# Sums of half activations in a hybrid attention block: joined parts, and parts that follow one and two pieces later

## The chip, the cores and the metric

The kernel runs on one core of a Trainium2 chip. The metric is the device time of one execution in microseconds (us). Five engines work side by side, each through its own queue in order: TensorE (PE, matmuls; its weight loads are PEld), VectorE (DVE), ScalarE (ACT), GpSimd (POOL) and SyncE (SP). SP issues the loads of weights, POOL most other transfers. Line numbers such as L147 are those of the kernel before.

## The reference

One layer of a decoder block on 512 positions of width 2048, all in float32. Cut to what matters:

```
h    = rms_norm(x, norm_g)
proj = h @ w_in                       # q, kv, gate logits, z_a, uv, z_b, merge logits
o_a  = nsa_attention(q, kv, gates) * silu(z_a)
u, v = split(gelu(uv))
o_b  = u * (tril(w_s) @ layer_norm(v) + b_s) * silu(z_b)
g_a, g_b = split(sigmoid(merge_logits))
merged = g_a * (o_a @ w_up_a) + g_b * (o_b @ w_up_b)
x    = x + merged @ w_out
x    = x + sigmoid(x @ w_ple_gate) * (p @ w_ple)
out  = rms_norm(x, final_g)
```

## The kernel before

**Two parts per number.** TensorE multiplies float32 operands rounded to fp32r. To keep the accuracy, each operand is split into a high part (the rounded value, a cast by ScalarE, `high`, L141) and a low part (what is left, a subtraction by VectorE, `low`, L147), and each product is three matmuls: high x high, high x low, low x high.

**Two kinds of jobs.** A plain job (kinds "N" and "T") multiplies the activations with a block of weights in pieces, one piece for each 128 rows of weights (in u and wo). A job of kind "S" multiplies two column blocks of 512 at once with seven products of halves instead of eight. These need sums and differences of halves: of the weights (VectorE, L240, in the stream) and of the activations. With first and second half of the 2048 channels (k1, k2) and of each 512 positions' tile (lo_t, hi_t, 256 wide), the activation sums are s1 = (k1, hi_t) + (k2, hi_t), s2 = s1 - (k1, lo_t), s3 = (k1, lo_t) - (k1, hi_t), and s4 = (k2, lo_t) - s2. s1 lies as product "5" in `ob_h`, s2 as "6" in `ob_l`, s4 as "3" in two tiles `s40` and `s41`; s3 is staged in a tile `stage`, stored to DRAM (`s3_dram`) and loaded later over the (hi_t) halves of the activations.

**The stream.** `gemm` (L288) is a generator that emits the matmuls of all jobs in order: pl, kc, vc, k, vs, vw, q and za, then u0, u1 (plain), vn, zb, m0 to m3, ua (S), ub, wo0, wo1 (plain), wo2 (S), pg (plain). At the head of each piece it calls `flush()`, which runs what was put on the list `deferred`, then `split_to`, which emits the high parts of the weights up to three pieces ahead and the low parts two pieces ahead, and then `pop()`, which takes items from the queue `background`: `state["pops"]` items per piece, on average. What runs during `flush` and is put on `deferred` again comes at the next piece's head. `fill(n)` advances the stream by n quarter pieces, `finish(name)` to the end of a job, with a flush.

**The work around the change.** The sums are background items, first while u0 and u1 run (on h), and again while wo0 and wo1 run (on merged). `sum_chunk(c)` (L1201) makes s1, s2 and s3 of two of the eight channel tiles, c from 0 to 3, in seven items; `s4_chunk(c)` (L1246) s4 in three. All read high and low parts of the activations as separate operands. In the first use the items of `sum_chunk` alternate with those of `oa_chunk` (L1172), which makes the sums for the job ua from the attention's output and stores them to `oa_dram` through a ring of three tiles (tag "hs"). Parts are made inside the item that makes the sum: `split`, or `high` and then `low` in the next item. Rings of tiles in the pool `quad`: "s1" (two tiles, the sums), "ls" (three: `oas`, `stage`, and the low parts of S jobs), "hs" (three: `oa`, and the high parts of S jobs).

Rates: two items per piece in u (L1269), 1.5 for the s4 items behind them (L1302), 1.75 in wo (L1472). Between the first items the masked spatial weights are made: `wn` is loaded, turned by TensorE (L1282), masked (L1283) and stored (L1286), and `bn` is turned (L1288).

In wo0's end VectorE adds the result to x (L675); TensorE turns the sums (L1490) for the job pg.

Of the kernel before, what the change touches and what calls it, by code (L numbers as in the profile page):

```python
# [4 lines left out]

# [1 line left out]

# [6 lines left out]
F32 = mybir.dt.float32  # L14
F32R = mybir.dt.float32r
# [48 lines left out]
def kernel(ctx: ExitStack, tc: tile.TileContext, x, p, norm_g, w_in,  # L64
# [54 lines left out]
    def act_h(k, sl=slice(None)):  # L119
        return act_part("h", k, sl)  # L120
# [1051 lines left out]
    def oa_chunk(c):  # L1172

        f1, f2 = o32[:, c], o32[:, c + 4]
        lo_t, hi_t = slice(0, 256), slice(256, 512)
        w = {}

        def put(src, i, n):
            o = quad["pool"].tile([P, 2, S], F32R, tag="hs", name="oa", bufs=3)[:, :, :256 * n]
            split(o[:, 0], o[:, 1], src, 0.5)  # L1180
            for j in range(n):
                nc.gpsimd.dma_start(oa_dram[:, i + j, :, c], o[:, :, 256 * j:256 * j + 256])
# [18 lines left out]
    def sum_chunk(c):  # L1201

        lo_t, hi_t = slice(0, 256), slice(256, 512)
        k1, k2 = slice(2 * c, 2 * c + 2), slice(2 * c + 8, 2 * c + 10)
        h11, l11, h21, l21 = (a(k1, t) for t in (lo_t, hi_t) for a in (act_h, act_l))
        h12, l12, h22, l22 = (a(k2, t) for t in (lo_t, hi_t) for a in (act_h, act_l))
        w = {}

        def op(a, b, f):
            nc.vector.tensor_tensor(out=w["t"], in0=a.bitcast(F32) if a is not None else w["t"],  # L1210
                                    in1=b.bitcast(F32) if b is not None else w["t"], op=f)

        def first():
            w["t"] = quad["pool"].tile([P, 2, 256], F32, tag="s1", name="sum", bufs=2)
            op(h21, h22, ALU.add)
            op(None, l21, ALU.add)

        def s1():
            op(None, l22, ALU.add)
            split(sum_part("5", k1, lo_t), sum_part("5", k1, hi_t), w["t"])  # L1220

        def s2():
            op(None, h11, ALU.subtract)
            op(None, l11, ALU.subtract)
            high(sum_part("6", k1, lo_t), w["t"])

        def s2_low():
            low(sum_part("6", k1, lo_t), sum_part("6", k1, hi_t), w["t"])

        def s3():  # L1230
            w["t"] = quad["pool"].tile([P, 2, 256], F32, tag="s1", name="sum", bufs=2)
            op(h11, h21, ALU.subtract)
            op(None, l11, ALU.add)

        def s3_high():
            op(None, l21, ALU.subtract)
            w["o"] = quad["pool"].tile([P, 2, S], F32R, tag="ls", name="stage", bufs=3)
            high(w["o"][:, :, lo_t], w["t"])

        def s3_low():  # L1240
            low(w["o"][:, :, lo_t], w["o"][:, :, hi_t], w["t"])
            for i, t in enumerate((lo_t, hi_t)):
                nc.gpsimd.dma_start(s3_dram[:, i, k1], w["o"][:, :, t])
        return [first, s1, s2, s2_low, s3, s3_high, s3_low]

    def s4_chunk(c):  # L1246
        k1, k2 = slice(2 * c, 2 * c + 2), slice(2 * c + 8, 2 * c + 10)
        lo_t, hi_t = slice(0, 256), slice(256, 512)
        w = {}

        def first():
            t = w["t"] = quad["pool"].tile([P, 2, 256], F32, tag="s1", name="sum", bufs=2)
            h12, l12, h, l = (a.bitcast(F32) for a in (act_h(k2, lo_t), act_l(k2, lo_t),
                                                       sum_part("6", k1, lo_t), sum_part("6", k1, hi_t)))
            nc.vector.tensor_tensor(out=t, in0=h12, in1=h, op=ALU.subtract)
            nc.vector.tensor_tensor(out=t, in0=t, in1=l, op=ALU.subtract)
            w["l"] = l12
# [12 lines left out]
    wn, ws = (quad["pool"].tile([P, 8, P], F32, tag="ls", name=n, bufs=3) for n in ("wn", "ws"))  # L1270
    tri = mix["pool"].tile([P, P], F32, tag="v", name="tri", bufs=2)
    bn = mix["pool"].tile([8, P], F32, tag="v", name="bn", bufs=2)
    nc.sync.dma_start(wn, sgu_w.rearrange("g t s -> t g s"))
    nc.sync.dma_start(bn, sgu_b)
    nc.gpsimd.memset(tri, 1.0)
    nc.gpsimd.affine_select(out=tri, in_=tri, pattern=[[1, P]], compare_op=ALU.is_ge, fill=0.0,
                            base=0, channel_multiplier=-1)
    fill(16)
    for hf in range(2):
        b = bank("s", "ps_w")  # L1280
        for j in range(4):
            nc.tensor.transpose(b[:, j * P:j * P + P], wn[:, 4 * hf + j], ident)  # L1282
        nc.vector.tensor_tensor(out=ws[:, 4 * hf:4 * hf + 4], in0=b.rearrange("p (g t) -> p g t", g=4),  # L1283
                                in1=tri.unsqueeze(1).to_broadcast([P, 4, P]), op=ALU.mult)
        fill(4)
    nc.gpsimd.dma_start(ws_dram, ws)  # L1286
    b = bank("s", "ps_b")
    nc.tensor.transpose(b[:, :8], bn, ident[:8, :8])  # L1288
    nc.vector.tensor_copy(sgu_bt, b[:, :8])
# [292 lines left out]
```

## Time and profile before

| what | us |
|---|---|
| median of 3 runs (1576.57 to 1576.93) | 1576.73 |
| the profiled execution's own time | 1576.64 |
| its span, first to last instruction | 1574.9 |
| TensorE busy | 1559.2 |
| VectorE busy | 1108.6 |
| ScalarE busy | 743.7 |
| GpSimd busy | 230.7 |

The page gives for each engine its busy time, then the chain of work that ended last, followed back from the end. Other views: busy time by stage (a window in us from the span's start, its length, and for each engine busy time and count of instructions, then the granted TensorE clock, the share of time that the DMA engines were busy, and GB/s); waits (who waited for whom: total us, times, longest); timelines (start, us, engine, line, operation, output<-input, count, and in brackets the idle time before it and what ended it); groups of instructions by line (count, busy us, mean ns, idle time before); and transfers (count, KB each, median us from issue to landing). u0 and u1 run from 490.7 to 579.4 us of the span, vn to 656.5, zb to 732.7; wo0 and wo1 from 1217.3 to 1309.8, then wo2.

### The profile page before, as it was taken

What the parts mean: (1) busy time and instruction counts of PE and PEld (TensorE: products, weight loads), DVE (VectorE), ACT (ScalarE), POOL (GpSimd) and SP (SyncE); (2) the same over time, 40 slices, a digit from 0 to 9 for tenths busy, and PEclk for the clock granted to TensorE, in tenths of its full rate; (3) what the DMA queues carried; (4) which work ended last, traced back from release to release, by engine and by line L of the source; (5) the groups of instructions that cost most, each with busy time, mean ns of one, the idle gap of its engine ahead of it and who ended that gap; (6) DMA issues with size and microseconds to landing.
All of it is one profiled execution on the core that took longest, in us unless ns stands there. A gap on an engine that the chain in (4) does not pass through costs nothing.

```text
span 1574.9 us, 20483 instructions
## 1 busy us (share of the span) xinstructions
PE 1559.2 (99%) x7534; PEld 1304.6 (83%) x7534; DVE 1108.6 (70%) x1795; ACT 743.7 (47%) x1307; POOL 230.7 (15%) x344
## 2 busy tenths in 40 slices
PE   9999999999999999999999999999999999999997
PEld 7889988888888888888888888888888878888886
DVE  6543358889887787878887777777576687843336
ACT  7433346666664445445544444454322334433334
POOL 1200000101112420001121212110032111011111
PEclk9999999999999999999999999999999999999999
DMA  9422431112114992526473737674733476573443
GB/s 326 120 80 84 113 81 43 53 41 54 46 50 124 264 315 87 200 64 230 142 254 120 253 103 267 241 269 155 291 112 94 133 249 205 171 283 99 156 147 134
DMA packets 152916, 246.16 MB, mean 156 GB/s; under 512 B 8280, under 2 KB 78576, under 8 KB 150384
## 3 DMA queue, kind: packets, MB, share of 16 engines
q1 hardware_dynamic: 114768, 150.00, 30.6%
q0 software_dynamic: 37904, 94.49, 17.7%
q8 instruction: 59, 0.97, 0.2%
q14 instruction: 41, 0.34, 0.1%
q10 hardware_dynamic: 144, 0.36, 0.1%
HBM read 197.11 MB, written 47.71 MB: 155 GB/s over the span
## 4 chain that ended last, share of the span: by engine, by line
PE 90%; DVE 6%; ACT 2%; DMA 1%; issue 1%; SPq 0%; DVEq 0%; POOL 0%; ACTq 0%; POOLq 0%
PE ps_m L311 6%; PE ps_m L312 6%; PE ps_m L313 6%; PE ps_pg L351 3%; PE ps_pg L349 3%; PE ps_pg L350 3%; PE ps_za L337 2%; PE ps_za L339 2%; PE ps_t L1019 2%; PE ps_za L338 2%; PE ps_ub L351 2%; PE ps_ub L350 2%; PE ps_ub L349 2%; PE ps_wo L313 2%; PE ps_ua L313 2%; PE ps_zb L313 2%
## 5 line engine op out<-in xcount | busy, mean ns | idle before, releaser
L147 DVE TENSOR_TENSOR lo<-raw,hi 128x512 fp32r<-128x512 f32 (+1 forms) x280 | 195.1, 702 | 174.4 <-PE ps_pg L350 81.7
L141 ACT CAST hi<-raw 128x512 fp32r<-128x512 f32 (+1 forms) x280 | 168.7, 610 | 251.9 <-PE ps_pg L351 95.9
L147 DVE TENSOR_TENSOR ls<-b,hs 128x1024 fp32r<-128x1024 f32 x160 | 195.9, 1224 | 105.8 <-ACT hs L141 105.0
L141 ACT CAST hs<-b 128x1024 fp32r<-128x1024 f32 x160 | 168.0, 1053 | 191.1 <-PE ps_m L313 88.3
L141 ACT CAST hs<-raw 128x1024 fp32r<-128x1024 f32 x64 | 67.5, 1054 | 82.7 <-PE ps_m L313 35.2
L311 PE MATMUL ps_m<-hs,act_h 128*128 128x512 f32 x256 | 100.5, 393 | 0.0
L312 PE MATMUL ps_m<-ls,act_h 128*128 128x512 f32 x256 | 99.7, 389 | 0.0
L313 PE MATMUL ps_m<-hs,act_l 128*128 128x512 f32 x256 | 99.6, 389 | 0.0
L147 DVE TENSOR_TENSOR ls<-raw,hs 128x1024 fp32r<-128x1024 f32 x64 | 78.3, 1223 | 14.6 <-ACT hs L141 14.5
L141 ACT CAST pth<-ps_t 128x512 fp32r<-128x512 f32 (+1 forms) x88 | 48.0, 546 | 65.5 <-PE ps_t L1019 65.2
L240 DVE TENSOR_TENSOR b<-b,b 128x1024 f32<-128x1024 f32 x64 | 78.0, 1219 | 0.0
L240 DVE TENSOR_TENSOR b<-raw,b 128x1024 f32<-128x1024 f32 x64 | 78.0, 1218 | 0.0
L980 ACT ACTIVATE prob<-prob,st 128x512 f32<-128x512 f32 (+3 forms) x128 | 70.7, 556 | 4.0 <-DVE st L971 3.8
L147 DVE TENSOR_TENSOR ptl<-ps_t,pth 128x512 fp32r<-128x512 f32 (+1 forms) x88 | 56.3, 639 | 21.1 <-ACT pth L141 20.3
L971 DVE CUSTOM_DVE_ANT_0 prob<-ps_s,b 128x512 f32<-128x512 f32 (+3 forms) x128 | 56.3, 486 | 10.0 <-PE ps_s L968 9.8
L313 PEld LDWEIGHTS ps_m<-hs,act_l 128*128 128x128 f32 x256 | 48.1, 188 | 10.1
L311 PEld LDWEIGHTS ps_m<-hs,act_h 128*128 128x128 f32 x256 | 48.1, 188 | 9.8
L312 PEld LDWEIGHTS ps_m<-ls,act_h 128*128 128x128 f32 x256 | 48.1, 188 | 9.7
L337 PE MATMUL ps_za<-act_h,hi 128*128 128x512 f32 x128 | 55.8, 436 | 0.0
L337 PE MATMUL ps_q<-act_h,hi 128*128 128x512 f32 x128 | 53.6, 419 | 0.0
L1019 PEld LDWEIGHTS ps_t<-ident,prob 128*128 128x128 f32 x320 | 39.7, 140 | 13.9 <-DVE ptl L147 2.8
L350 PE MATMUL ps_wo<-lo,act_h 128*128 128x512 f32 x128 | 49.9, 390 | 1.2 <-DVE lo L147 1.2
(511 smaller groups left out, 4361.9 us busy)
## 6 DMA issues: line engine op xcount, KB each, us to landing
raw<-in_w_in_dram SPq DMA_DIRECT2D x116, 512.0 KB, 3.7
b<-in_w_in_dram SPq DMA_DIRECT2D x48, 512.0 KB, 5.6
raw<-in_w_ple_gate_dram SPq DMA_DIRECT2D x32, 512.0 KB, 3.6
raw<-in_w_out_dram SPq DMA_DIRECT2D x24, 512.0 KB, 3.8
raw<-in_w_up_b_dram SPq DMA_DIRECT2D x16, 512.0 KB, 3.7
oa_d<-oa POOLq DMA_DIRECT2D x28, 256.0 KB, 3.6
gate<-keep POOLq DMA_DIRECT2D x24, 256.0 KB, 3.8
xt<-in_x_dram SPq DMA_DIRECT2D x4, 1024.0 KB, 10.1
```

The source lines that it names most:

```text
L141: nc.scalar.copy(hi, src)
L147: nc.vector.tensor_tensor(out=lo, in0=src, in1=hi.bitcast(F32), op=ALU.subtract)
L240: nc.vector.tensor_tensor(out=b[o], in0=b[x], in1=b[y], op=ALU.subtract)
L311: nc.tensor.matmul(o, ah, hi[:, i], start=st, stop=False, skip_group_check=go)
L312: nc.tensor.matmul(o, ah, lo[:, i], start=False, stop=False, skip_group_check=go)
L313: nc.tensor.matmul(o, al, hi[:, i], start=False, stop=sp, skip_group_check=go)
L337: nc.tensor.matmul(ps, hi[:, j], ah, start=st, stop=False)
L349: nc.tensor.matmul(o, ah[:, sl], hi[:, j], start=st, stop=False)
L350: nc.tensor.matmul(o, ah[:, sl], lo[:, j], start=False, stop=False)
L351: nc.tensor.matmul(o, al[:, sl], hi[:, j], start=False, stop=sp)
L980: nc.scalar.activation(sl, sl, AF.Exp, bias=st[:, 0, j, hh:hh + 1], scale=-1.0, accum_out=st[:, 1, j, hh:hh + 1])
L1019: nc.tensor.transpose(b[:, (2 * e + hh) * P:(2 * e + hh + 1) * P], pts[hh][:, c:c + P], ident)
```

## The change

Sums are made from joined parts: `whole` first adds high and low parts of the k1 halves into one tile of tag "ls", and s1, s2 and s3 start from there. In wo a chunk has four items, the last of which makes s4 from s2's sum while it is still whole; in u `sum_chunk` has three items and `s4_chunk` two. The parts of a sum are made by `parts_later`: the high part at the head of the next piece, the low part (and the store of `stage`) at the head of the one after. In `oa_chunk` the high part is made in the item, the low part and the store at the next head. The queue in u is two `oa` items and one sum item in turn, 1.6 a piece, then 1.2 for the s4 items; in wo it is 0.7. Four flushes follow the last item in u. `wn` and `ws` are each two tiles of half the size in the rings of the pool `mix`, stored in two halves, and `bn` lies in a tile of the ring "s1" and is turned before `wn`.

```diff
@@ oa_chunk
         def put(src, i, n):
             o = quad["pool"].tile([P, 2, S], F32R, tag="hs", name="oa", bufs=3)[:, :, :256 * n]
-            split(o[:, 0], o[:, 1], src, 0.5)
-            for j in range(n):
-                nc.gpsimd.dma_start(oa_dram[:, i + j, :, c], o[:, :, 256 * j:256 * j + 256])
+            split(o[:, 0], o[:, 1], src, 0.5, later=True)
+
+            def store():
+                for j in range(n):
+                    nc.gpsimd.dma_start(oa_dram[:, i + j, :, c], o[:, :, 256 * j:256 * j + 256])
+            deferred.append(store)
@@ new helpers
+    def parts_later(hi, lo, src, then=None):
+
+        def second():
+            low(hi, lo, src)
+            if then:
+                then()
+
+        def first():
+            high(hi, src)
+            deferred.append(second)
+        deferred.append(first)
+
+    def new_sum():
+        return quad["pool"].tile([P, 2, 256], F32, tag="s1", name="sum", bufs=2)
@@ sum_chunk
-        return [first, s1, s2, s2_low, s3, s3_high, s3_low]
+        def whole():
+            t = w["t"] = quad["pool"].tile([P, 4, 256], F32, tag="ls", name="whole", bufs=3)
+            add(t[:, 0:2], act_h(k1, hi_t), act_l(k1, hi_t))
+            add(t[:, 2:4], act_h(k1, lo_t), act_l(k1, lo_t))
+
+        def s1():
+            o = w["1"] = new_sum()
+            add(o, w["t"][:, 0:2], act_h(k2, hi_t))
+            add(o, o, act_l(k2, hi_t))
+            parts_later(sum_part("5", k1, lo_t), sum_part("5", k1, hi_t), o, lambda: w.update(ready=True))
+
+        def s23():
+            o, t = new_sum(), w["t"]
+            w["2"] = o
+            sub(o, w["1"], t[:, 2:4])
+            sub(t[:, 2:4], t[:, 2:4], t[:, 0:2])
+            parts_later(sum_part("6", k1, lo_t), sum_part("6", k1, hi_t), o)
+            st = quad["pool"].tile([P, 2, S], F32R, tag="ls", name="stage", bufs=3)
+
+            def store():
+                for i, t in enumerate((lo_t, hi_t)):
+                    nc.gpsimd.dma_start(s3_dram[:, i, k1], st[:, :, t])
+            parts_later(st[:, :, lo_t], st[:, :, hi_t], t[:, 2:4], store)
+
+        def s4():
+            assert w["ready"]
+            o = w["1"]
+            sub(o, act_h(k2, lo_t), w["2"])
+            add(o, o, act_l(k2, lo_t))
+            parts_later(sum_part("3", k1, lo_t), sum_part("3", k1, hi_t), o)
+        return [whole, s1, s23] + fourth * [s4]
@@ s4_chunk
         def second():
-            nc.vector.tensor_tensor(out=w["t"], in0=w["t"], in1=w["l"], op=ALU.add)
-            high(sum_part("3", k1, lo_t), w["t"])
-
-        def third():
-            low(sum_part("3", k1, lo_t), sum_part("3", k1, hi_t), w["t"])
-        return [first, second, third]
-
-    for pair in zip_longest(*([f for c in range(4) for f in g(c)] for g in (oa_chunk, sum_chunk))):
-        background.extend(f for f in pair if f)
-    state["pops"] = 2
+            o = w["o"]
+            add(o, o, act_l(k2, lo_t))
+            parts_later(sum_part("3", k1, lo_t), sum_part("3", k1, hi_t), o)
+        return [first, second]
+
+    oa_items = [f for c in range(4) for f in oa_chunk(c)]
+    sum_items = [f for c in range(4) for f in sum_chunk(c, False)]
+    for i in range(12):
+        background.extend(oa_items[2 * i:2 * i + 2] + sum_items[i:i + 1])
+    state["pops"] = 1.6
@@ behind it
+    for hf in range(2):
+        nc.sync.dma_start(wn[hf], sgu_w[4 * hf:4 * hf + 4].rearrange("g t s -> t g s"))
     nc.sync.dma_start(bn, sgu_b)
...
     fill(16)
+    b = bank("s", "ps_b")
+    nc.tensor.transpose(b[:, :8], bn, ident[:8, :8])
+    nc.vector.tensor_copy(sgu_bt, b[:, :8])
+    fill(4)
...
     while background:
         fill(1)
+    for _ in range(4):
+        flush()
...
-    state["pops"] = 1.5
+    state["pops"] = 1.2
...
-    for f in (sum_chunk, s4_chunk):
-        for c in range(4):
-            background.extend(f(c))
-    state["pops"] = 1.75
+    for c in range(4):
+        background.extend(sum_chunk(c))
+    state["pops"] = 0.7
```

More of the change, by code (lines that the diff above doesn't have):

```diff
@@ L1204, in sum_chunk @@
+    def new_sum():
+        return quad["pool"].tile([P, 2, 256], F32, tag="s1", name="sum", bufs=2)
+    def sum_chunk(c, fourth=True):
         k1, k2 = slice(2 * c, 2 * c + 2), slice(2 * c + 8, 2 * c + 10)
-        h11, l11, h21, l21 = (a(k1, t) for t in (lo_t, hi_t) for a in (act_h, act_l))
-        h12, l12, h22, l22 = (a(k2, t) for t in (lo_t, hi_t) for a in (act_h, act_l))
         w = {}
-        def op(a, b, f):
-            nc.vector.tensor_tensor(out=w["t"], in0=a.bitcast(F32) if a is not None else w["t"],
-                                    in1=b.bitcast(F32) if b is not None else w["t"], op=f)
@@ L1213, in first @@
[L1213 to L1216, printed above, removed]
-        def s1():
[L1219 to L1243, printed above, removed]
@@ L1271 @@
[L1271 to L1273 removed]
+            o = w["o"] = new_sum()
+            sub(o, act_h(k2, lo_t), sum_part("6", k1, lo_t))
+            sub(o, o, sum_part("6", k1, hi_t))
+        def second():
+            o = w["o"]
+            add(o, o, act_l(k2, lo_t))
+            parts_later(sum_part("3", k1, lo_t), sum_part("3", k1, hi_t), o)
@@ new lines, in s4_chunk @@
+        return [first, second]
[4 more added lines that the diff above has]
+    state["pops"] = 1.6
+    wn, ws = ([mix["pool"].tile([P, 4, P], F32, tag=tags[i], name=n, bufs=2 if tags == "vv" else 1) for i in range(2)]
+              for n, tags in (("wn", "vv"), ("ws", ("g0", "g1"))))
+    tri = mix["pool"].tile([P, P], F32, tag="w", name="tri")
```

27 lines of the change are left out of this document (10 added, 17 removed).

## The prediction

> **What bounds the kernel now.** I read the page first, then busy time by stage, the waits of TensorE, and the timelines around those waits. The page:
>
> ```profile
> span 1574.9 us, 20483 instructions
> ...
> PE 90%; DVE 6%; ACT 2%; DMA 1%; issue 1%; SPq 0%; DVEq 0%; POOL 0%; ACTq 0%; POOLq 0%
> ```
>
> TensorE sets the end, and the order of its instructions stays (three small groups of transposes excepted). So the change can only win what TensorE now loses in the stages where the sums are made: u0 and u1, with their tail in vn (first use), and wo0 and wo1 (second use). The table of stages (window, its length, then each engine's busy time):
>
> ```profile
> 490.70:579.40 88.70, 88.70 (x395) 73.10 (x394) 73.14 (x124) 38.38 (x67) 30.95 (x45) 1.00 0.94 273
> 579.40:656.50 77.10, 76.48 (x337) 62.99 (x336) 61.60 (x61) 38.04 (x45) 7.40 (x12) 1.00 0.51 157
> 656.50:732.70 76.20, 76.20 (x338) 63.08 (x337) 60.09 (x58) 37.00 (x43) 4.32 (x8) 1.00 0.43 139
> 1217.30:1309.80 92.50, 91.21 (x418) 75.34 (x418) 72.45 (x110) 33.21 (x56) 15.87 (x19) 1.00 0.66 213
> ```
>
> u has no idle time at all. vn (77.10) is 0.9 longer than zb (76.20), which has the same matmuls. wo has 1.3 idle. The waits of TensorE in 480 to 735 us and in 1200 to 1400 us are these two:
>
> ```profile
> PE ps_vn L312 <- DVE ls L147: 0.6, 1, 0.6
> ...
> PE ps_wo L350 <- DVE lo L147: 1.2, 1, 1.2
> ```
>
> A busy matmul is 0.39 but the next starts 0.23 later, so the price of a stall is its step from start to start less 0.23. TensorE's timeline at the three places where it loses time:
>
> ```profile
> 590.28 0.39 PE L311 MATMUL ps_vn<-hs,act_h 128*128 128x512 f32 x1
> 591.30 0.50 PE L312 MATMUL ps_vn<-ls,act_h 128*128 128x512 f32 x1 [0.62 <-DVE ls L147]
> 591.64 0.40 PE L313 MATMUL ps_vn<-hs,act_l 128*128 128x512 f32 x1
> ...
> 1266.74 1.33 PE L1490 MATMUL ps_x<-ident,x 128*128 128x128 f32 x8
> ...
> 1273.37 1.03 PE L1490 MATMUL ps_x<-ident,x 128*128 128x128 f32 x8
> ...
> 1281.06 0.39 PE L349 MATMUL ps_wo<-hi,act_h 128*128 128x512 f32 x1
> 1282.65 0.50 PE L350 MATMUL ps_wo<-lo,act_h 128*128 128x512 f32 x1 [1.21 <-DVE lo L147]
> 1282.98 0.39 PE L351 MATMUL ps_wo<-hi,act_l 128*128 128x512 f32 x1
> ```
>
> vn: 1.02 - 0.23 = 0.79, and 0.34 - 0.23 = 0.11 in the step after it: 0.90. The first transposes of x take 1.33 where the next eight take 1.03: 0.30. wo1: 1.59 - 0.23 = 1.36, and 0.33 - 0.23 = 0.10: 1.46. Together 2.66 us. That is all there is to win.
>
> Who is late at these places? VectorE, behind the sums (L1210, L1255 to L1264), and it is late because it waits inside them: each sum's high part is cast by ScalarE at once, and the low part, next in VectorE's queue, waits for that. VectorE, then ScalarE:
>
> ```profile
> 588.28 0.69 DVE L147 TENSOR_TENSOR s<-sum,s 128x512 fp32r<-128x512 f32 x1 [0.69 <-ACT s L141]
> 588.89 1.22 DVE L240 TENSOR_TENSOR b<-b,b 128x1024 f32<-128x1024 f32 x1
> 590.02 2.50 DVE L147 TENSOR_TENSOR ls<-b,hs 128x1024 fp32r<-128x1024 f32 x2
> ...
> 1278.84 0.69 DVE L1210 TENSOR_TENSOR sum<-sum,act_l 128x512 f32<-128x512 f32 x1
> 1280.71 1.29 DVE L147 TENSOR_TENSOR x2t<-ps_x,x2t 128x512 fp32r<-128x512 f32 x2 [1.17 <-ACT x2t L141]
> 1281.91 0.68 DVE L147 TENSOR_TENSOR lo<-raw,hi 128x512 fp32r<-128x512 f32 x1
> ...
> 1279.57 0.62 ACT L141 CAST ob_l<-sum 128x512 fp32r<-128x512 f32 x1 [2.21 <-DVE sum L1210]
> 1280.09 1.07 ACT L141 CAST x2t<-ps_x 128x512 fp32r<-128x512 f32 x2
> ```
>
> At 1279.57 ScalarE has idled 2.21 for a sum; the two x2t casts stand behind it, VectorE waits 1.17 for those, and `lo`, which TensorE needs at 1281.3, starts at 1281.91. At 588.28 the low part of `s` comes after 0.69 of waiting, then L240 and two `ls`, the second of which TensorE needs at 590.5.
>
> **The change part by part.** First, the instructions. A chunk had 11 VectorE sums (8 in `sum_chunk`, 3 in `s4_chunk`). In wo it now has 8 (two each in `whole`, `s1`, `s23`, `s4`); in u it has 9, since `s4_chunk` keeps its 3. With four chunks: 8 fewer in u, 12 fewer in wo. The price of one, and of the low and high parts, whose number stays:
>
> ```profile
> L1210 DVE TENSOR_TENSOR sum<-sum,act_l 128x512 f32<-128x512 f32 x20 | 13.8, 690 | 0.4
> L147 DVE TENSOR_TENSOR lo<-raw,hi 128x512 fp32r<-128x512 f32 x31 | 21.2, 685 | 0.0
> L141 ACT CAST hi<-raw 128x512 fp32r<-128x512 f32 x29 | 17.5, 618 | 8.2 <-PE ps_u L351 5.5 <-issue 1.6 <-ACT hi L141 1.0
> ```
>
> 8 x 0.69 = 5.5 us of VectorE in u, 12 x 0.69 = 8.3 in wo.
>
> Second, the waits. `parts_later` puts the cast at the head of the next piece of the stream and the low part at the head of the one after. VectorE's waits for parts, first from u and vn, then from wo (where `ob_h` has the same row):
>
> ```profile
> DVE ob_h L147 <- ACT ob_h L141: 2.8, 4, 0.7
> DVE s L147 <- ACT s L141: 2.8, 4, 0.7
> DVE stage L147 <- ACT stage L141: 0.7, 1, 0.7
> ...
> DVE stage L147 <- ACT stage L141: 2.8, 4, 0.7
> DVE s L147 <- ACT s L141: 1.4, 2, 0.7
> ```
>
> 6.3 us in u, 7.0 in wo. The length of a piece, from u's matmuls (128 of this line, four to a piece):
>
> ```profile
> L349 PE MATMUL ps_u<-hi,act_h x128: 389/389/504, 491.0 to 578.7; 128*128 128x512 f32 x128
> ```
>
> 87.7 / 127 x 4 = 2.76 us, against a cast of 0.62: the part is there long before VectorE asks. The casts no longer wait on ScalarE either, because the sum was issued a piece earlier. One exception: after the last item of u four flushes follow each other at once, so up to three parts still wait, 0.7 each; `lo` is two pieces (5.5) ahead of TensorE, which hides it.
>
> So VectorE gets back 11.8 us in u and 15.3 in wo, in stages where it was busy 73.1 of 88.7 and 72.5 of 92.5 beside its waits. In wo1 the `lo` that came 0.6 late and held TensorE for 1.36 comes several us earlier: I take the whole 1.46. The adds of x (L675) no longer stand in a queue that runs late, so the transposes find them done: 0.30. In vn the tail goes: the items at 1.6 a piece are done after 36 / 1.6 = 22.5 pieces (before: 52 / 2 = 26), and the eight s4 items at 1.2 take 6.7 more, 29.2 of the 32 pieces of u0 and u1 (before: 26 + 8 = 34, two of them in vn). What is late next there is VectorE's own `ls` work, 3 x 1.22 = 3.7 us in each two pieces of 5.5, which keeps up in zb without a stall: 0.90. Sum: -2.66.
>
> Third, what is moved. On POOL's queue the stores of `oa` and `stage` come one and two pieces later, and the ws store is two of half the size; on SP's queue wn is two loads, ahead of weights that wait for a buffer anyway. The prices of the stores, from the page, from the burst of weights at 564 us, and from a quiet stretch at 1286 us; then the weights of wo2's burst, and one issue of two stores:
>
> ```profile
> oa_d<-oa POOLq DMA_DIRECT2D x28, 256.0 KB, 3.6
> ...
> s_d<-stage POOLq DMA_DIRECT2D x2, 256.0 KB, 7.4
> ...
> s_d<-stage POOLq DMA_DIRECT2D x2, 256.0 KB, 3.1
> ...
> b<-in_w_out_dram SPq DMA_DIRECT2D x8, 512.0 KB, 11.8
> ...
> 505.21 1.43 POOL L1182 DMA_DIRECT2D oa_d<-oa  x2 [5.52 <-DVE oa L149]
> ```
>
> Where the change adds a wait: an `oa` tile (tag hs, three of them) is held a piece longer, 2.76 until its low part, 0.7 for that, 1.4 to issue, and the landing: h = 4.9 + landing. The next high part of `oa` waits on ScalarE for such a tile, with the casts of the weights queued behind it, and TensorE waits for those. Sixteen tiles go through three places in 16 / 3 x h; the items give them 22.5 x 2.76 = 62.1 us, and `lo` is 5.5 ahead, so TensorE pays when 5.33 h is over 67.6, at a mean landing of 7.8. At 3.6, 5.33 h is 45.3: cost nothing, with 22 us of cover. At 11.8 for every store it is 89.0: cost 21.4. I take the 3.6, which is the median of these very stores in u, and keep the other end for a rival.
>
> A rule speaks against this. The Trainium skill, "DMA: Bandwidth & Descriptors", section "Issuing engines are not separate DMA queues", says that transfers started by different engines end on the same 16 DMA engines and interleave. The trace agrees: the same kind of store lands in 7.4 us inside a burst and in 3.1 outside. By that rule, taken to its end, every store of u would land as in a burst: h would be 12.3 and 5.33 h 65.6, which is still under 67.6, so the sum would stay, with 2 us of cover.
>
> In wo the last `stage` store now falls into the burst. Its buffer is wanted again by the third `ls` of wo2, four pieces (11.0 us) later; 1.4 to issue and 7.4 to land fit. If it took 11.8, it would be 2.2 late, but the four adds of x and an L240 stand ahead of that `ls`: cost nothing.
>
> The small transposes: ps_b goes ahead of ps_w and now reads a tile of the sums' ring; its 4 KB load is third instead of second on SP, with four pieces to land. From none to one piece late: bound 0 to 2.8, taken 0.
>
> **Sum.** The profiled execution took 1576.64 us (span 1574.9); 1576.64 - 2.66 = 1573.98. The median is 1576.73, 0.09 above: 1574.1.
>
> **The rivals.**
> (1) The stalls shrink but stay. vn's stall also has the gelu of u1 on ScalarE ahead of its casts, wo1's also the x2t casts, and neither moves. For: both stand in the chain. Against: zb has no stall under the same load. If only the waits' share of the vn and wo1 stalls goes, about half: -1.3, 1575.4.
> (2) Slower: the ring of `oa` tiles becomes the bound of u. It decides from a mean landing of 7.8, and makes the kernel slower by over 0.2% (3.15 us) from one of 8.9. At 11.8 throughout: 1576.73 - 2.66 + 21.4 = 1595.5. DMA at 0.94 in u speaks for it, the median of 3.6 against. The Trainium skill, "TensorE: Matmul & The Clock Gate", Part 1, says that after an idle window of some 3.4 us the array runs at half its clock, by which such stalls would cost more than their length; the granted clock above is 1.00 after 0.6 and 1.2 of idle, and no run here shows longer ones.
> (3) Nothing to speak of: the freed VectorE time lies in slack and the stalls come back somewhat later, within 1576.0 to 1579.8; 1577 as a value. Against: the rows name VectorE as the releaser.
> (4) Faster by over 0.2%: needs 3.15 us, and the stalls that I find sum to 2.66. Only a loss that the rows don't show could give it: 1573.0.
>
> **How the numbers follow.** Forecast 0.66, its own range 1573.6 to 1574.9 (the vn stall half kept at the upper end); (1) 0.12; (2), with like rings and queues, 0.12; (3) 0.05; (4) 0.05. Within 0.2%, about what a measurement of this kernel can tell from no change, lie the forecast, (1) and (3): 0.83. Faster 0.05, slower 0.12. The range 1573.5 to 1577.0 leaves out (2), most of (4) and part of (3).
>
> **What would show it.** Right: no wait of TensorE for `ls` near 591 and for `lo` near 1282; eight transposes of x at 1.03 both times; vn at 76.2 and wo some 1.8 shorter; VectorE's waits for ob_h, s and stage gone but for the four flushes. Wrong: ScalarE waiting before `oa` for a landing, a new wait of TensorE in u, or VectorE waiting before `whole` or the third `ls` of wo2.

## The result and the profile after

The changed kernel takes 1573.77 us (median of 18 runs, 1573.31 to 1574.44), the kernel before, on the same chip, 1576.74 (18 runs, 1576.48 to 1577.28). The ratio is 0.9981, 95% interval 0.9974 to 0.9988: 3.0 us less, 0.19%. The forecast was 1574.1. The profiled execution took 1573.90 us (before: 1576.64), 2.74 less.

The page of the changed kernel (span; busy time of the engines; the chain that ended last by engine). Line numbers after the change are other ones: `low` is L146, `high` L140, all sums L1207.

```profile
span 1572.2 us, 20465 instructions
...
PE 1559.0 (99%) x7534; PEld 1306.0 (83%) x7534; DVE 1096.4 (70%) x1775; ACT 747.1 (48%) x1307; POOL 230.7 (15%) x345
...
PE 96%; DVE 2%; ACT 1%; issue 0%; POOL 0%; DVEq 0%; POOLq 0%; ACTq 0%
```

TensorE's share of the chain went from 90 to 96%, VectorE's from 6 to 2. TensorE's own work is the same (1559.0 and 1559.2), so it is idle time that went. By stage (u, vn, zb, wo; columns as before: window, its length, then PE, PEld, DVE, ACT, POOL):

```profile
490.80:579.50 88.70, 88.70 (x395) 73.12 (x395) 73.41 (x122) 42.47 (x72) 32.26 (x48) 1.00 0.95 273
579.50:655.70 76.20, 76.20 (x338) 63.10 (x337) 57.28 (x54) 35.92 (x41) 6.60 (x11) 1.00 0.51 159
...
1216.50:1307.10 90.60, 90.60 (x417) 75.40 (x416) 64.27 (x98) 34.99 (x56) 15.74 (x19) 1.00 0.70 219
```

vn is 76.20 long (77.10 before) and without idle time, wo 90.60 (92.50). The waits of TensorE in these stretches have no row left. The two groups of transposes of x, which took 1.33 and 1.03:

```profile
1265.88 1.03 PE L1508 MATMUL ps_x<-ident,x 128*128 128x128 f32 x8
1272.21 1.03 PE L1508 MATMUL ps_x<-ident,x 128*128 128x128 f32 x8
```

The stalls show the same. Summed over 480 to 735 and 1200 to 1400 us, what TensorE's steps have over the usual 0.23 fell from 4.24 to 1.58: 2.66 us, against 2.73 of span. The medians differ by 0.2 to 0.3 more, which is the spread of the runs.

VectorE's waits in the changed kernel, first from u and vn, then from wo:

```profile
DVE ls L146 <- ACT hs L140: 6.7, 5, 3.4
DVE oa L148 <- ACT oa L142: 3.5, 5, 0.9
...
DVE lo L146 <- ACT s L140: 1.4, 1, 1.4
...
DVE lo L146 <- ACT ob_h L140: 0.7, 1, 0.7
...
DVE lo L146 <- PE ps_wo L349: 10.5, 7, 2.0
...
DVE lo L146 <- ACT ob_h L140: 2.1, 3, 0.7
DVE lo L146 <- ACT stage L140: 1.4, 2, 0.7
```

The rows in which `ob_h`, `s` and `stage` waited for their own high parts are gone. What VectorE waits for in wo is mainly TensorE itself (10.5 us, for a tile of weights to come free; 4.4 before): it is early where it was late. Some waits for casts stay, 3.5 us in wo, under the name of `lo`, and cost TensorE nothing.

On ScalarE one wait for a landing appeared, in the window 490 to 592, and the stores of `oa` land later than the 3.6 that the prediction took (last column):

```profile
ACT oa L142 <- DMA oa_d<-oa: 1.2, 1, 1.2
```

```profile
oa_d<-oa POOLq DMA_DIRECT2D x28, 256.0 KB, 5.0
```

### The profile page after: what moved, and what is told of

It reads as the page before. It is cut to its first block, busy times and chain, and to the rows that moved or that the text cites. A ratio compares the mean times of both kernels' runs of the same rounds, so it can differ in the third digit from the quotient of the medians.

```text
span 1572.2 us, 20465 instructions
## 1 busy us (share of the span) xinstructions
PE 1559.0 (99%) x7534; PEld 1306.0 (83%) x7534; DVE 1096.4 (70%) x1775; ACT 747.1 (48%) x1307; POOL 230.7 (15%) x345
## 4 chain that ended last, share of the span: by engine, by line
PE 96%; DVE 2%; ACT 1%; issue 0%; POOL 0%; DVEq 0%; POOLq 0%; ACTq 0%
PE ps_m L310 6%; PE ps_m L311 6%; PE ps_m L312 6%; PE ps_pg L350 3%; PE ps_pg L348 3%; PE ps_pg L349 3%; PE ps_za L336 2%; PE ps_za L338 2%; PE ps_t L1018 2%; PE ps_za L337 2%; PE ps_u L348 2%; PE ps_u L349 2%; PE ps_wo L350 2%; PE ps_ub L350 2%; PE ps_ub L349 2%; PE ps_u L350 2%
## 5 line engine op out<-in xcount | busy, mean ns | idle before, releaser
L146 DVE TENSOR_TENSOR lo<-raw,hi 128x512 fp32r<-128x512 f32 (+1 forms) x280 | 195.4, 703 | 190.6 <-PE ps_pg L349 84.0
L140 ACT CAST hi<-raw 128x512 fp32r<-128x512 f32 (+1 forms) x280 | 169.6, 610 | 279.5 <-PE ps_pg L350 94.6
L146 DVE TENSOR_TENSOR ls<-b,hs 128x1024 fp32r<-128x1024 f32 x160 | 195.9, 1225 | 111.8 <-ACT hs L140 111.0
L140 ACT CAST hs<-b 128x1024 fp32r<-128x1024 f32 x160 | 168.1, 1052 | 198.4 <-PE ps_m L312 86.1
L140 ACT CAST hs<-raw 128x1024 fp32r<-128x1024 f32 x64 | 67.4, 1054 | 83.8 <-PE ps_m L312 35.8
L146 DVE TENSOR_TENSOR ls<-raw,hs 128x1024 fp32r<-128x1024 f32 x64 | 78.3, 1223 | 15.1 <-ACT hs L140 15.1
L140 ACT CAST pth<-ps_t 128x512 fp32r<-128x512 f32 (+1 forms) x88 | 48.0, 545 | 65.6 <-PE ps_t L1018 65.3
L146 DVE TENSOR_TENSOR ptl<-ps_t,pth 128x512 fp32r<-128x512 f32 (+1 forms) x88 | 56.2, 639 | 21.1 <-ACT pth L140 20.2
L1018 PE MATMUL ps_t<-ident,prob 128*128 128x128 f32 x320 | 49.5, 273 | 1.3 <-DVE ptl L146 1.2
```

What stands on the lines that cost most here:

```text
L140: nc.scalar.copy(hi, src)
L146: nc.vector.tensor_tensor(out=lo, in0=src, in1=hi.bitcast(F32), op=ALU.subtract)
L1018: nc.tensor.transpose(b[:, (2 * e + hh) * P:(2 * e + hh + 1) * P], pts[hh][:, c:c + P], ident)
```

## The experiments

"Lost" is what TensorE's steps have over 0.23 (0.11 between transposes), from its timeline, for steps more than 0.13 longer than that; the smaller excesses add up to 1.6 to 2.3 us in every kernel. Every ratio is to the kernel before on the same chip.

| kernel | us | ratio, 95% interval | lost in u, vn | lost in wo |
|---|---|---|---|---|
| before | 1576.74 | 1 | 0.79 | 1.61 |
| changed | 1573.77 | 0.9981 (0.9974 to 0.9988) | 0 | 0 |
| joined sums, parts at once | 1574.24 | 0.9984 (0.9975 to 0.9993) | 0 | 0 |
| separate sums, parts later | 1574.16 | 0.9985 (0.9976 to 0.9994) | 0.27 | 0 |
| change in u alone | 1575.83 | 0.9996 (0.9987 to 1.0005) | 0 | 1.74 |
| change in wo alone | 1574.82 | 0.9988 (0.9980 to 0.9997) | 0.72 | 0 |
| before, faster rates in u | 1577.49 | 1.0005 (0.9996 to 1.0014) | 1.06 | 1.78 |
| `oa` parts and stores at once | 1573.93 | 0.9982 (0.9974 to 0.9991) | 0 | 0 |
| two `oa` tiles | 1573.81 | 0.9982 (0.9973 to 0.9991) | 0 | 0 |
| new order alone | 1579.52 | 1.0019 (1.0010 to 1.0028) | 4.98 | 0 |
| 20 sums more in wo | 1574.04 | 0.9983 (0.9974 to 0.9992) | 0 | 0 |
| 40 sums more in wo | 1584.83 | 1.0051 (1.0038 to 1.0065) | 0 | 9.83 |
| before, wo's order alone | 1574.90 | 0.9988 (0.9979 to 0.9997) | 0.75 | 0 |
| new order alone, u slower | 1579.38 | 1.0019 (1.0010 to 1.0028) | 4.24 | 0.74 |

### Each half of the change alone

The changed kernel with the parts of the sums made at once (those of `oa` too, by the diff shown with the ring below; all else as changed):

```diff
     def parts_later(hi, lo, src, then=None):
-        def second():
-            low(hi, lo, src)
-            if then:
-                then()
-        def first():
-            high(hi, src)
-            deferred.append(second)
-        deferred.append(first)
+        high(hi, src)
+        low(hi, lo, src)
+        if then:
+            then()
```

> The changed kernel with the parts of each sum, and those of oa, made at once inside the item (cast, then low part): joined sums and the new rates alone. My theory (VectorE's lateness, of which 20 sums fewer and the waits for casts are two shares): the tail in vn is gone by the rates, so the 0.90 us there goes; in wo VectorE still has 12 sums (8.3 us) less, so the lo near 1282 comes in time and 1.46 + 0.30 go too: 1574.1, some 0.998 of before. Rival A (only the waits matter, since the casts stand before others on ScalarE): the wo stalls stay, only 0.9 goes: 1575.8. VectorE's waits for ob_h, ob_l, stage and s are back by either, at 0.7 each.

Measured: 1574.24 us, ratio 0.9984 (0.9975 to 0.9993), and TensorE has no stall. VectorE's waits for parts are back in u and vn:

```profile
DVE s L146 <- ACT s L140: 2.8, 4, 0.7
DVE ob_h L146 <- ACT ob_h L140: 2.7, 4, 0.7
```

They cost nothing here. The other half: separate sums (11 a chunk in u, 10 in wo) in the new order, with the parts later.

```diff
-            add(t[:, 0:2], act_h(k1, hi_t), act_l(k1, hi_t))
-            add(t[:, 2:4], act_h(k1, lo_t), act_l(k1, lo_t))
+            o = w["1"] = new_sum()
+            add(o, act_h(k1, hi_t), act_h(k2, hi_t))
+            add(o, o, act_l(k1, hi_t))
...
-            sub(o, w["1"], t[:, 2:4])
-            sub(t[:, 2:4], t[:, 2:4], t[:, 0:2])
+            sub(o, w["1"], act_h(k1, lo_t))
+            sub(o, o, act_l(k1, lo_t))
+            sub(t, act_h(k1, lo_t), act_h(k1, hi_t))
+            add(t, t, act_l(k1, lo_t))
+            sub(t, t, act_l(k1, hi_t))
```

> The changed kernel with the sums made from separate high and low parts again (8 per chunk in u, so 11 with s4; 10 in wo), parts one and two pieces later as changed. My theory: VectorE has 8 x 0.69 more work in u and wo than in the changed kernel, but no waits of 0.7; TensorE loses nothing at 591 and 1282: 1574.1. Rival B (only the number of sums matters): wo keeps its 1.46 us stall, 1575.5. Rival A: as mine.

Measured: 1574.16 us, ratio 0.9985 (0.9976 to 0.9994), one stall of 0.27 near 561 us (for `lo`). So with the new order and rates, which both kernels have, each half alone takes nearly all of the gain; together they don't add up to more, because nothing is left to gain. The times of these two and of the changed kernel lie within each other's intervals; the stalls tell them apart.

### Each place alone

The change in u alone (wo as before), and in wo alone (u as before), each as a difference to the changed kernel (`old_sum_chunk` and `old_s4_chunk` are the functions of the kernel before, `new_sum_chunk` is that of the changed one):

```diff
-    for c in range(4):
-        background.extend(sum_chunk(c))
-    state["pops"] = 0.7
+    for f in (old_sum_chunk, old_s4_chunk):
+        for c in range(4):
+            background.extend(f(c))
+    state["pops"] = 1.75
```

> The change in u0 and u1 alone; wo as before (seven and three items, 1.75 per piece). My theory: 0.90 us less, from vn: 1575.8; the stalls near 1267 and 1282 stay at 0.30 and 1.46. If the 0.3 us that the changed kernel won beyond the 2.66 comes from u, 1575.5.

```diff
-        background.extend(sum_chunk(c))
+        background.extend(new_sum_chunk(c))
```

(with `oa_chunk`, `sum_chunk`, `s4_chunk`, the rates and `wn` of u as before.)

> The change in wo0 and wo1 alone; u as before. My theory: 1.76 us less: 1575.0; TensorE still waits for ls near 591 for 0.6. If the 0.3 us beyond the 2.66 comes from wo, 1574.7.

Measured: 1575.83 and 1574.82 us, 0.74 and 1.75 less than the kernel before on that chip (1576.57). The prediction's split was 0.90 and 1.76. By time alone the 0.74 can't be told from no change (its interval takes in 1); that it is vn's stall is read from the waits. The waits of TensorE that stay, of the kernel with u alone, and then of the one with wo alone:

```profile
PE ps_wo L349 <- DVE lo L146: 0.6, 1, 0.6
PE ps_x L1575 <- DVE x L674: 0.5, 2, 0.3
```

```profile
PE ps_vn L312 <- DVE ls L147: 0.6, 1, 0.6
```

The two places are independent: each keeps the loss, or near it, that it has when the other is unchanged. But wo's loss with the old code (1.74) isn't made of the same stalls as before: 0.98 at the transposes of x and 0.76 at `lo`, where it was 0.24 and 1.37. The stage starts a little earlier there, and the stalls moved; that the sum stayed looks like chance.

### Rates and order without the rest

The kernel before with u's items faster, so that they end in u as in the changed kernel:

```diff
-    state["pops"] = 2
+    state["pops"] = 2.2
...
-    state["pops"] = 1.5
+    state["pops"] = 2
```

> The kernel before with faster rates in u alone: 2.2 items per piece instead of 2, and 2 instead of 1.5 for the s4 items, so that the tail ends some two pieces before vn (52 / 2.2 + 12 / 2 = 29.6 pieces). My theory: the stall at 591 in vn goes (0.90), but VectorE, 81.4 busy of 97 us and with its waits nearly full, falls behind in u: 10% more items per piece is over 1.5 us per 5.5 us; lo is late near the end of the items and u loses 1 to 4 us: 1575.8 to 1580. Rival (the tail alone made the stall, u has room): 1575.8. The wo stalls stay by both.

Measured: 1577.49 us, ratio 1.0005 (0.9996 to 1.0014): no gain. The stall at 591 went, and others came: 0.64 at 544 and 545, 0.42 at 581. An end in time isn't enough for vn.

Next, grouping, order and rates as changed, but sums separate and parts at once: neither half, only the new places (in wo 40 sums instead of 44). Its code is that of the two halves' diffs put together.

> The changed kernel with separate sums (8 per chunk in u and 11 with s4, 10 in wo) and parts made at once: neither fewer sums nor later parts, only the new grouping of the items, their order (a chunk's s4 behind its s3) and the new rates. My theory: VectorE in wo has 40 of the 44 sums of before and all its waits for casts, so it runs late at the end of wo0 again, and the stalls near 1266 and 1282 are back with 1 to 1.7 us together; vn's is gone by the rates: 1575.0 to 1575.8. Rival C (the order of the items alone does it, since s4 no longer falls behind the sums of all chunks): no stall, 1574.0.

Measured: 1579.52 us, ratio 1.0019 (1.0010 to 1.0028): slower than before, and above both expectations. In wo no stall is left, in u one of 3.4 us is new. ScalarE and then VectorE around it:

```profile
538.55 1.28 ACT L543 ACT_TABLE_LOAD   x1
539.84 2.06 ACT L543 ACTIVATE u<-ps_u 128x512 f32<-128x512 f32 x4
...
542.28 0.45 ACT L142 ACTIVATE oa<-o 128x256 fp32r<-128x256 f32 x1
```

```profile
542.76 0.42 DVE L148 SCALAR_TENSOR_TENSOR oa<-o,oa 128x256 fp32r<-128x256 f32 x1 [2.76 <-ACT oa L142]
...
545.16 1.42 DVE L1204 TENSOR_TENSOR whole<-whole,act_l 128x512 f32<-128x512 f32 x2
546.49 0.68 DVE L146 TENSOR_TENSOR ob_l<-sum,ob_l 128x512 fp32r<-128x512 f32 x1
547.26 0.69 DVE L146 TENSOR_TENSOR stage<-whole,stage 128x512 fp32r<-128x512 f32 x1
547.87 0.68 DVE L146 TENSOR_TENSOR lo<-raw,hi 128x512 fp32r<-128x512 f32 x1
```

The gelu of u0 holds ScalarE for 3.3 us (the load of its table and four activations). A high part of `oa` stands behind it, and VectorE waits 2.76 for that. Then come, in one item, five sums, then two low parts, and only then the `lo` that TensorE wants from 545.2 on: it starts at 547.87. The same place in the changed kernel (VectorE's timeline):

```profile
536.58 0.69 DVE L1207 TENSOR_TENSOR sum<-sum,whole 128x512 f32<-128x512 f32 x1
537.30 0.69 DVE L1207 TENSOR_TENSOR whole<-whole 128x512 f32<-128x512 f32 x1
538.90 0.42 DVE L148 SCALAR_TENSOR_TENSOR oa<-o,oa 128x256 fp32r<-128x256 f32 x1 [0.91 <-ACT oa L142]
539.25 0.69 DVE L146 TENSOR_TENSOR lo<-raw,hi 128x512 fp32r<-128x512 f32 x1
```

Here the wait behind the gelu is 0.91, the item with s2 and s3 is two sums long, and `lo` follows the wait at once. This is what the two halves do in u: shorten the item, and take VectorE's waits out from between. Either is enough at this place: neither kernel with one half has the stall.

The stall costs more than its length. TensorE's timeline in the kernel with the new order alone, and the rows of the stall and of the slow stretch behind it by windows (TensorE's busy time is the first value behind the length, the granted clock the third from the end):

```profile
544.96 0.39 PE L348 MATMUL ps_u<-hi,act_h 128*128 128x512 f32 x1
548.61 0.50 PE L349 MATMUL ps_u<-lo,act_h 128*128 128x512 f32 x1 [3.27 <-DVE lo L146]
```

```profile
546.03:549.44 3.41, 0.83 (x4) 0.70 (x5) 3.29 (x7) 1.67 (x4) 1.45 (x2) 1.00 0.41 109
549.44:552.86 3.42, 3.42 (x10) 2.64 (x9) 3.24 (x6) 1.13 (x2) 1.44 (x2) 0.50 1.01 272
```

From 549.4 to 552.9 a matmul starts every 0.43 us instead of every 0.23, at a granted clock of 0.50: 1.6 us on top of 3.4.

The same kernel with u's items at 1.4 a piece, nearly the 26 pieces that the kernel before took for them:

```diff
-    state["pops"] = 1.6
+    state["pops"] = 1.4
...
-    state["pops"] = 1.2
+    state["pops"] = 1.5
```

> As the run with the new order alone (separate sums, parts at once), but the items in u at 1.4 a piece instead of 1.6, and the items of the fourth sums at 1.5 instead of 1.2: 36 / 1.4 = 25.7 pieces and 8 / 1.5 = 5.3, together 31.0 of 32. Theory A (the stall of 3.4 us at 548.6 came from the spacing of the same work in 22.5 pieces instead of 26): with 25.7 pieces it goes, and the time is 1574.0 to 1575.3. Theory B (it came from what coincides: the gelu of u0 on ScalarE, table load and four activations of together 3.2 us, stands ahead of a high part that VectorE waits for, and a long item, five sums, follows ahead of the low part that TensorE needs): at 1.4 another item may stand there, so the stall at the end of u0 shrinks or grows with which item it is, but TensorE still loses 0.5 us or more in u or vn, 1574.8 to 1577.5. Wo has no stall under either.

Measured: 1579.38 us, above the ranges of both theories, ratio 1.0019 (1.0010 to 1.0028). The stall at the end of u0 is gone, as theory A has it, and two others stand in vn, as theory B has it; its range fell short because the clock dropped again (1.6) and wo lost 0.74. The waits of TensorE in u and vn, and its busy time and clock around the longer one:

```profile
PE ps_vn L311 <- DVE ls L146: 2.1, 2, 1.5
```

```profile
578.42:581.84 3.42, 1.88 (x8) 1.02 (x7) 3.39 (x4) 1.79 (x2) 0.00 (x0) 1.00 0.61 237
581.84:585.25 3.41, 3.41 (x10) 2.63 (x9) 2.73 (x4) 0.95 (x2) 0.00 (x0) 0.50 0.00 0
```

With the whole work in VectorE's queue, the slower rate only moved the stall from one coincidence to another. In wo, whose code is that of the kernel with the new order alone, 0.74 came back at the first transposes of x, where that kernel had nothing: the `lo` and the adds of x stand in the other order there. So without either half it is chance which item meets which wait, in wo too.

### Wo: order or amount

The kernel before with one edit:

```diff
-    for f in (sum_chunk, s4_chunk):
-        for c in range(4):
-            background.extend(f(c))
+    for c in range(4):
+        background.extend(sum_chunk(c) + s4_chunk(c))
     state["pops"] = 1.75
```

> The kernel before with one edit in wo: the three items of a chunk's fourth sum follow the seven items of its first three sums, instead of standing behind all four chunks. Number of sums, time of the parts and rate (1.75 items a piece) stay as before. Theory A (spacing and order alone keep VectorE ahead in wo, as the run with the new order alone suggests): both stalls of wo go, 1.76 us less of TensorE time, vn's 0.90 stays: about 1.75 us under the kernel before, some 1574.9. Theory B (the amount of work and the waits for parts decide, the new order alone does not carry over to the old rate): wo keeps its stalls within 0.5 us, 1576.2 to 1576.9. In between: the stalls move to another piece, and the text says which.

Measured: 1574.90 us, ratio 0.9988 (0.9979 to 0.9997), as theory A has it: wo has no stall, vn keeps its own. The number of sums and the waits for parts are what they were (VectorE's waits in 1217 to 1310 us, 6.9 together; before 7.0), but they stand elsewhere. VectorE's timeline of this kernel, where the kernel before waited 1.17 for `x2t` at 1280.71:

```profile
DVE ob_h L147 <- ACT ob_h L141: 2.7, 4, 0.7
DVE s L147 <- ACT s L141: 1.4, 2, 0.8
DVE stage L147 <- ACT stage L141: 1.4, 2, 0.7
DVE ob_l L147 <- ACT ob_l L141: 1.4, 2, 0.7
```

```profile
1278.14 0.69 DVE L147 TENSOR_TENSOR ob_l<-sum,ob_l 128x512 fp32r<-128x512 f32 x1 [0.69 <-ACT ob_l L141]
1278.75 1.28 DVE L147 TENSOR_TENSOR x2t<-ps_x,x2t 128x512 fp32r<-128x512 f32 x2
1279.95 0.68 DVE L147 TENSOR_TENSOR lo<-raw,hi 128x512 fp32r<-128x512 f32 x1
```

And ScalarE's cast for this `ob_l`, which was at 1279.57:

```profile
1277.49 0.62 ACT L141 CAST ob_l<-sum 128x512 fp32r<-128x512 f32 x1 [2.17 <-DVE sum L1210]
```

The cast stands ahead of the casts of `x2t` in both kernels. But between one group of two `x2t` and the next, VectorE's queue had five sums and has three here; two of them come ahead of the first group, where there is time. So the cast is 2.1 us earlier (0.4 of it because the stage itself is), `x2t` waits for nothing, and `lo` starts at 1279.95 instead of 1281.91. One reordered line has all of wo's gain. Neither half of the change was run in wo at the old order, so what a half would do there without the new order isn't shown.

Then the amount. The changed kernel with five sums of a chunk made twice in wo (20 more), and three times (40 more); the result is the same:

```diff
-            add(t[:, 0:2], act_h(k1, hi_t), act_l(k1, hi_t))
+            for _ in range(1 * fourth + 1):
+                add(t[:, 0:2], act_h(k1, hi_t), act_l(k1, hi_t))
```

(and so for the second sum of `whole`, and the first of `s1`, `s23` and `s4`; `2 * fourth + 1` in the other kernel.)

> The changed kernel; in wo five of a chunk's eight sums are made twice with the same result (13 per chunk instead of 8, 20 more in all, some 14 us of VectorE). My theory: in the changed kernel VectorE waits some 21 us in wo behind the start of the items (for TensorE, for casts and on issue), so these 14 us fit; TensorE loses 0 to 0.5 us near the end of wo0, where the adds of x stand: 1573.8 to 1574.3. Rival (VectorE's cover is no more than what the change gave back): 1575.3 or more.

> As the last, but each of the five three times (18 per chunk, 40 more in all, some 27 us of VectorE). My theory: 27 is over the 21 of cover; TensorE waits for lo and for the adds of x in wo, and loses some 6 us, 3 to 9: 1577 to 1583. Rival (VectorE's load is not what TensorE waited for, but the casts on ScalarE were): parts still come later, so no stall: 1574.

Measured: 1574.04 us, ratio 0.9983 (0.9974 to 0.9992), and 1584.83, ratio 1.0051 (1.0038 to 1.0065), more than the 1577 to 1583 expected. The busy time in wo with 20 more (VectorE is the third value after the length), and the waits of TensorE with 40 more:

```profile
1216.50:1307.10 90.60, 90.60 (x418) 75.37 (x417) 77.03 (x118) 33.56 (x56) 16.38 (x19) 1.00 0.69 220
```

```profile
PE ps_wo L349 <- DVE lo L146: 6.9, 7, 1.8
```

With 77.03 us of work VectorE is busier than in the kernel before (72.45), and TensorE waits for nothing; with some 14 us more it loses 9.8. So VectorE is what TensorE waits for once there is too much, but the amount that the kernel before had is not too much in this order.

### The ring of `oa` tiles

`oa` with its parts and stores at once, all else as changed:

```diff
-            split(o[:, 0], o[:, 1], src, 0.5, later=True)
-
-            def store():
-                for j in range(n):
-                    nc.gpsimd.dma_start(oa_dram[:, i + j, :, c], o[:, :, 256 * j:256 * j + 256])
-            deferred.append(store)
+            split(o[:, 0], o[:, 1], src, 0.5)
+            for j in range(n):
+                nc.gpsimd.dma_start(oa_dram[:, i + j, :, c], o[:, :, 256 * j:256 * j + 256])
```

> The changed kernel with the parts and stores of oa made at once again; the sums' parts stay later. My theory: VectorE's waits for oa rise by some us, an oa tile is held 2.76 us less and ScalarE does not wait for a landing; TensorE loses nothing either way: the same as the changed kernel, 1573.8 within 0.3. Rival (the deferral of oa is a part of the gain): 1574.3 or more.

Measured: 1573.93 us, ratio 0.9982 (0.9974 to 0.9991), no stall. VectorE's wait for `oa` is three times that of the changed kernel, and the stores land in 3.2 instead of 5.0; neither reaches TensorE:

```profile
DVE oa L148 <- ACT oa L142: 10.0, 12, 2.3
```

The changed kernel with two tiles in turn instead of three:

```diff
-            o = quad["pool"].tile([P, 2, S], F32R, tag="hs", name="oa", bufs=3)[:, :, :256 * n]
+            if len(oa_ring) < 2:
+                oa_ring.append(quad["pool"].tile([P, 2, S], F32R, tag="hs", name="oa", bufs=3))
+            o = oa_ring[oa_puts[0] % 2][:, :, :256 * n]
+            oa_puts[0] += 1
```

> The changed kernel with two oa tiles in turn instead of three. My theory of the ring: TensorE pays when 16 / 2 x h is over 67.6 us; with h = 4.9 + 5.0 (the landing's median in the changed kernel) that is 79.2 - 67.6 = 11.6 us: 1585, with ScalarE waiting before oa for landings. Rival (ScalarE and the leads hide more than I think): under 1577.

Measured: 1573.81 us, ratio 0.9982 (0.9973 to 0.9991): no loss, where the ledger of the prediction asked for one. ScalarE's waits in 490 to 592 us:

```profile
ACT oa L142 <- DMA oa_d<-oa: 10.4, 7, 2.6
...
ACT oa L142 <- DMA s_d<-stage: 4.4, 1, 4.4
```

ScalarE did wait for landings, 10.4 us in seven waits (and 4.4 in one put down to the store of `stage`), and the weights' casts behind it still came in time. The stores landed in 4.4. By the ledger 16 / 2 x (4.9 + 4.4) = 74.4, 6.8 over the 67.6 at which TensorE should pay. Since it paid nothing, h was, by the same ledger, at most 67.6 / 8 = 8.45, where the ledger has 9.3. The starts and ends in the timelines give h itself: from the start of an `oa` tile's high part to the end of its issues the sixteen tiles took 3.76 us on average, and 3.76 + 4.4 = 8.2.

## Why the prediction was right, and where not

**The sum.** All three stalls went, and their prices held: 2.66 of steps forecast, 2.66 measured, 2.73 of span. vn came to the 76.2 forecast, the transposes to 1.03 both times, wo to 1.90 less (some 1.8 forecast). The forecast of 1574.1 is 0.3 from the median, inside the spread of the runs.

**The instructions.** Twenty fewer on VectorE, as counted; in wo 72.45 - 64.27 = 8.2 us (8.3 forecast). Over the whole span VectorE's busy time fell by 12.2, not 13.8: 0.61 for each on average instead of the 0.69 that one takes. Where two neighbours on VectorE don't depend on each other, the second can start before the first has ended, and busy time counts the overlap once. VectorE's timeline of the changed kernel has two such sums in 1.29, so the second starts 0.60 after the first:

```profile
1265.86 1.29 DVE L1207 TENSOR_TENSOR whole<-act_h,act_l 128x512 f32<-128x512 f32 x2
```

The step from start to start would have been the better price, as it was for TensorE.

**The waits.** In u the forecast was up to three waits of 0.7 left, and 2.1 are there for the parts (`lo` behind `s`, 1.4, and once behind `ob_h`, 0.7). In wo 3.5 of 7.0 stayed, where none was forecast. VectorE reaches a `lo` there before ScalarE's cast is done; since it is early as a whole, the wait takes slack, and no wait of TensorE follows.

**Why VectorE was late in wo: the step that failed.** "It is late because it waits inside them", so that fewer sums and later parts (15.3 us) were taken as what removes the stalls of 1.46 and 0.30. The runs show less. The order alone removes both, with all 44 sums and 6.9 us of waits in place, and VectorE with more work than before stalls nothing. The 1.46 came of a coincidence: five sums between two groups of `x2t`, the last one's cast ahead of the `x2t` casts on ScalarE. The changed kernel has the new order too (a chunk's fourth sum behind its first three), and the prediction's sum has no term for it. So that wo's number came out is in part luck: the stalls were priced in full, and an edit that the prediction did not count is enough to remove them. What the halves add is room: of the kernels that have one or both of them in wo, only the one with 40 sums more loses anything there, while of the two that have the new order and neither half one loses 0.74.

**vn.** The end of the items inside u was taken to be enough, beside the time given back. It is not alone (1577.49 with faster rates), and with neither half the new order and rates lose 4.98. Here the freed VectorE time does carry the gain, but half of it would do: either half brings the loss to 0.27 or less. That the new order and rates are dangerous without it the prediction didn't see. No run takes the other edits in u back (the four flushes, the halves of `wn` and `ws`, the place of `bn`) or has a half at the old order and rates, so whether those edits are needed isn't shown; by the run with neither half they aren't enough.

**The ring.** Cost nothing, as forecast, but not for the reason given. The landing was 5.0, not 3.6, so by the ledger 5.33 h would be 52.8; still under 67.6. The rest of h was too large: the 2.76 for a piece was added in full. ScalarE and VectorE in the changed kernel, the two parts of one tile:

```profile
531.34 0.62 ACT L142 ACTIVATE oa<-oas 128x512 fp32r<-128x512 f32 x1
```

```profile
532.53 0.69 DVE L148 SCALAR_TENSOR_TENSOR oa<-oas,oa 128x512 fp32r<-128x512 f32 x1
```

Here the low part starts 1.19 us behind the high part; over the sixteen tiles it is 1.49 on average (1.34 with two tiles, and 0.79 with the parts at once), and from the start of the high part to the end of the issues 3.86 (3.76), where the ledger has 4.9. With the measured times two tiles give 8 x 8.2 = 65, under the 67.6, so the ledger itself then says that they cost nothing. A head one piece later in the program is thus not a whole piece later on the engines. A possible reason, not tested: ScalarE waits for TensorE ahead of such casts (14.1 us in 14 waits of `hi` for `ps_u` in 490 to 592 us), so that they run late in their piece. Rival (2) was farther off than the ledger had it.

**The other rivals.** (1), stalls that shrink but stay, didn't come: the `x2t` casts that it names were a part of the chain in wo, but the new order takes the late sum out from ahead of them. (3), stalls that come back elsewhere, is what the faster rates and the new order alone did, and in small the kernel with the separate sums (0.27 near 561 us, where the kernel before loses nothing): the danger was real, and the changed kernel has none of it. Rival (2) also asked what a longer stall would cost; the last section has that. The two stores of `ws`, the load of `bn` and the later stores of `stage` left no wait of TensorE, as forecast.

## What to carry to other kernels

A stall behind an in-order engine names the engine, not the cause: before taking work away, see which items stand ahead of the late one, and whether another order of the same items removes it, which here was one line worth 1.8 us. Room on the engine (fewer or shorter items, results consumed a piece later) is worth having because it made coincidences cost less here, and once nothing waits any more, more of it brings nothing. A ledger of a ring's holding time should take the times between the engines' instructions from a timeline: here one step of the schedule was 2.76 us on paper and 1.49 on the engines.

## What the runs showed of the hardware

The granted clock dropped to a half behind a stall, for 3.41 us each time: after a wait of 3.27 us (new order alone) and after one of 1.54 (the same with u slower; the rows are above). It did not drop after a wait of 1.79 in the kernel with 40 more sums. That wait, and the two windows that it lies in:

```profile
1280.19 0.50 PE L349 MATMUL ps_wo<-lo,act_h 128*128 128x512 f32 x1 [1.79 <-DVE lo L146]
```

```profile
1275.90:1279.31 3.41, 2.50 (x16) 1.87 (x14) 3.34 (x6) 0.90 (x2) 0.07 (x1) 1.00 0.18 68
1279.31:1282.73 3.42, 2.54 (x11) 2.12 (x12) 3.35 (x6) 0.29 (x1) 1.31 (x2) 1.00 0.76 207
```

So the length of the wait alone doesn't decide; where it falls does. In both traces with a drop, the changes of the clock lie a whole number of steps of 3.413 us apart: with the new order alone the first rise is at 6.72 us, the drop at 549.44 (159 steps later) and the rise at 552.86 (160). The windows above are these steps, in the kernel with 40 more sums counted from its first rise at 6.14. The windows ahead of the two drops have 0.83 and 1.88 us of TensorE's work, so 2.58 and 1.54 of idle time. The wait of 1.79 is cut by a border, 0.91 on one side and 0.88 on the other, and neither window brings a drop; the most idle time in one window without a drop, in that kernel, is 1.40 (1255.42 to 1258.83 us). If the idle time of one window decides, as these rows suggest, the border lies between 1.40 and 1.54 of 3.41 us here. The Trainium skill, "TensorE: Matmul & The Clock Gate", Part 1, says that the gate watches a free-running window of about 3.4 us; the steps of 3.413 us in these traces agree with it. Its rule to avoid idle gaps of more than some 3.4 us is too wide here: one of 1.54 was enough.
